# A two-layer hybrid trunk on one core: mixers in small parts between the projection matmuls, TensorE in program order

## The chip, the cores and the metric

The kernel runs on one core of a Trainium2 chip. The metric is the device time of one execution in microseconds, the median of three runs. A separate execution is recorded by the profiler; all views below come from it.

## The reference

A trunk of two layers on 256 tokens of width 1024. Each layer normalises its input, multiplies it with one wide weight and cuts the product into the inputs of three mixers (softmax differential attention, an SSD state space mixer in chunks of 128, and gated linear attention, GLA, in chunks of 64); their outputs, side by side, go through the output weight, then an FFN and a gate on a side input `p`.

```
for i in range(DEPTH):                          # DEPTH = 2
    a = rms_norm(h, attn_norm[i])
    proj = a @ w_in[i]
    (da_q, da_k, da_v, ssd_z, ssd_xbc, ssd_dt,
     gla_q, gla_k, gla_v, gla_g, gla_lr) = jnp.split(proj, IN_SPLITS, axis=-1)
    y_da = diff_attention(da_q, da_k, da_v, ...)    # rms norm and rope on q, k; two softmaxes, a difference
    y_ssd = ssd_mixer(ssd_z, ssd_xbc, ssd_dt, ...)  # conv of 4 taps, silu, decays, states of 2 chunks
    y_gla = gla_mixer(gla_q, gla_k, gla_v, gla_g, gla_lr, ...)  # log-sigmoid gates, cumulative sums, states of 4 chunks
    mix = jnp.concatenate([y_da, y_ssd, y_gla], axis=-1)
    h = h + mix @ w_out[i]
    f = rms_norm(h, ffn_norm[i])
    h = h + (silu(f @ w_ffn_gate[i]) * (f @ w_ffn_up[i])) @ w_ffn_down[i]
    h = h + sigmoid(h @ ple_w_gate[i]) * (p[i] @ ple_w_proj[i])
```

## The kernel before

Every matrix product is done in two halves of precision: a weight tile is loaded by DMA (`load_w`, L195 to L218), ScalarE copies its rounded part (`wh`, L213), VectorE subtracts to get the rest (`wl`, L214), and TensorE (PE) does three matmuls per pair of tiles (high by high, high by low, low by high). Activations have two halves in the same way.

The work is a list of units, one weight tile each. A layer has 19 input units in the order of the table `PLAN` (q, z, x, k, gq, gk, gv, sg, v, ple: the slices of `proj`; x0 to x3 are the inputs of SSD, gk and gq those of GLA), then four units o1 and two o2 for the output weight, 22 FFN units up with 16 down, and four gate units. In the input units with 512 columns per matmul the three matmuls stand on L836 to L838; z has 272 columns (L226 to L228); x and the output units use 256 columns (L244 to L246); the FFN is L238 and L240.

The mixers are Python generators: `da_gen` (attention), `ssd_gen`, `gla_gates_gen` and `gla_gen`. A `yield` ends a step; `step(S, names)` runs a generator to its next `yield`. `PLAN` names for each input unit the steps that are emitted whole ahead of the unit's own matmuls, and `PLAN_OUT` does so for the o1 units. The framework's scheduler then sets the order of each engine's instructions from these by its own costs, so PE's order in the program differs from the order of the text: mixer matmuls move between the projection matmuls. Each engine runs its list in order and waits at an instruction until what it needs is there.

PSUM's eight banks are divided: `NACC` = 5 for the accumulators of the units (`acc` tiles), 3 for the mixers (`pm` tiles).

Names that the text uses: `ssq` and L292, L295: the sum of squares and the PE matmul for the token norm. L706 to L712, L718: gates of GLA, `gk` and its cumulative sum. L553 to L558: convolution and SiLU of SSD. L651: the SSD product of B and C. L415 to L436: norm, rope and transposes of q and k (`qg`, `qh`, `ql`). L463 to L483: scores, their maximum `mx`, exponentials `e`. L755: GLA states (`gst`). L614 to L624: SSD outputs `xd`. L797, L805: GLA outputs.

Of the kernel before, what the change touches and what calls it, by code (L numbers as in the profile page):

```python
# [20 lines left out]
P = 128  # L21
# [12 lines left out]
BEFORE = False  # L34
NACC = 5
WSLOT = 2176
# [33 lines left out]


PLAN = [
    ('q0', ()),
# [7 lines left out]
    ('x3', ('gates',)),  # L81
    ('k0', ('gates', 'ssd', 'ssd')),
    ('k1', ('gates', 'ssd')),
    ('gk', ('da', 'da')),
    ('gv0', ('ssd', 'ssd')),
    ('gv1', ('gla', 'gla', 'da', 'da')),
    ('sg0', ('da', 'ssd')),
    ('sg1', ('gla', 'da')),
    ('v0', ('da', 'da', 'ssd', 'ssd')),
    ('v1', ()),  # L90
    ('ple', ('gla', 'da')),
]
PLAN_OUT = [('gla', 'da'), ('da',), (), ('da', 'da')]

# [13 lines left out]
def trunk_kernel(ctx: ExitStack, tc: tile.TileContext, a: dict):  # L108
    nc = tc.nc
    pe, dve, act, pool = nc.tensor, nc.vector, nc.scalar, nc.gpsimd  # L110

# [108 lines left out]
    split_at = []  # L220

    def product(out, pairs):

        n = len(pairs)
        for i, (sh, sl, mh, ml) in enumerate(pairs):
            pe.matmul(out, sh, mh, start=i == 0, stop=False)  # L226
            pe.matmul(out, sh, ml, start=False, stop=False)  # L227
            pe.matmul(out, sl, mh, start=False, stop=i == n - 1)  # L228

    def product_t(out, w, lo, x, ks, n, wide):  # L230


        if wide:

            pairs = list(zip(ks, w, strict=True))
            for p0 in range(0, len(pairs), 2):
                for k, (wh, _) in pairs[p0:p0 + 2]:
                    pe.matmul(out, wh[:, lo:lo + P], x[k], start=k == 0, stop=False)  # L238
                for k, (_, wl) in pairs[p0:p0 + 2]:
                    pe.matmul(out[:, :T], wl[:, lo:lo + P], x[k][:, :T], start=False, stop=k == n - 1)  # L240
            return
        for k, (wh, wl) in zip(ks, w, strict=True):
            sh, sl, hi = wh[:, lo:lo + P], wl[:, lo:lo + P], x[k][:, :T]
            pe.matmul(out, sh, hi, start=k == 0, stop=False)  # L244
            pe.matmul(out, sh, x[k][:, T:], start=False, stop=False)  # L245
            pe.matmul(out[:, :T], sl, hi, start=False, stop=k == n - 1)  # L246

    def gemm_t(blocks, x, wide=False, split=0, apart=False):
# [147 lines left out]
    def da_gen(i, S):  # L396
# [30 lines left out]
        for t in range(4):  # L427
# [9 lines left out]
            qk.append((qh, ql))  # L437
            if t == 1:
                yield
        yield  # L440
# [12 lines left out]
        for qb, heads in units:  # L453
            nh, nk = len(heads), P * (qb + 1)
            pb = [bank(), bank()]
            for j, hd in enumerate(heads):
# [3 lines left out]
                for n, (a_, b_) in enumerate(((0, 0), (0, 1), (1, 0))):  # L460
                    for c in range(2):
                        r = slice(64 * c, 64 * c + 64)
                        pe.matmul(pb[c][:, j * nk:(j + 1) * nk], q[a_][r, o + qb * P:o + (qb + 1) * P],  # L463
                                  k[b_][r, o:o + nk], start=j == 0 and n == 0, stop=False,
                                  skip_group_check=True)
            for c in range(2):
# [3 lines left out]
            if len(es_of) == 2:  # L470
                attn_t(es_of[0])
            mx = small("mx", [P, 2, 4])
# [33 lines left out]
        for qb in range(2):  # L506
            y = bank()
            for hd in range(4):
# [4 lines left out]
                else:  # L513
                    t = at[1 + hd // 2]
                    j = 2 * (hd % 2)
                    pe.matmul(o, t[:, j * P:(j + 1) * P], v[0][:, vs], start=True, stop=False)
                    pe.matmul(o, t[:, (j + 1) * P:(j + 2) * P], v[1][:, vs], start=False, stop=True)
            ys.append(head_norm(y))
            yield
# [41 lines left out]
    def ssd_gen(i, S):  # L561
# [18 lines left out]
        def decays(b):  # L580
            ms = []
            for g in range(2):
                pd = bank()
                for n, r in enumerate(rs[b][g]):
# [5 lines left out]
                                  cbm[:, o:o + P].unsqueeze(1).to_broadcast([P, 4, P]), ALU.mult)  # L590
                ms.append(m)
            return ms

# [14 lines left out]
        def rows(b, ms):  # L608
            py = bank()
            for hd in range(8):  # L610
                pe.matmul(py[:, hd * 64:(hd + 1) * 64], ms[hd // 4][:, (hd % 4) * P:(hd % 4 + 1) * P],
                          xdt[b][:, hd * 64:(hd + 1) * 64], start=True, stop=True)
            y = xd[b]
            dve.tensor_tensor(y, py, y, ALU.add)  # L614
# [37 lines left out]
        cbm = slot("cbm")  # L652
        dve.tensor_tensor(v3(cbm, 4), v3(pcb, 4), upper.unsqueeze(1).to_broadcast([P, 4, P]), ALU.mult)
        token_major(1)
        yield
# [7 lines left out]
        dve.tensor_tensor(v3(xe, 8), v3(xdt[0], 8), headed(ce[:, 0:8], 8), ALU.mult)  # L663
        m0 = decays(0)
        yield
# [5 lines left out]
        act.activation(st, pst, AF.Copy)  # L671
        rows(0, m0)
        rs.append(masked_dta(1))
# [7 lines left out]
        dve.tensor_tensor(xd[1], xd[1], ot, ALU.add)  # L681
        m1 = decays(1)
        yield
        rows(1, m1)
        yield
# [40 lines left out]
    def gla_gen(i, S):  # L726
# [5 lines left out]
        for j in range(2):  # L732
            for b in range(2):
                o = (2 * j + b) * P
                s = slice(j * T + b * P, j * T + (b + 1) * P)
                for e in range(2):
                    r = slice(64 * e, 64 * e + 64)
                    pe.matmul(pa[e][:, o:o + P], k[r, s], q[r, s], start=True, stop=True)
        for e in range(2):
            dve.copy_predicated(attm[e], gmask.unsqueeze(1).to_broadcast([P, 4, P]), v3(pa[e], 4))  # L740
# [11 lines left out]
        for j in range(2):  # L752
            for c in (0, 1, 2):
                b, r = c // 2, slice(64 * (c % 2), 64 * (c % 2) + 64)
                pe.matmul(pst[c][:, j * T:(j + 1) * T], kx[r, (2 * b + j) * P:(2 * b + j + 1) * P],  # L755
                          v[b][r, j * T:(j + 1) * T], start=True, stop=True)
        prev = [None]
        for c in range(3):
# [16 lines left out]
        for j in range(2):  # L775
            for b in range(2):
                o = (2 * j + b) * P
                for e in range(2):
                    hd = 2 * j + e
                    pe.matmul(po[e][:, o:o + P], attm[e][:, 2 * j + b], v[b][:, hd * P:(hd + 1) * P],  # L780
                              start=o == 0, stop=False, skip_group_check=True)
        for j in range(2):
            for c in range(1, 4):
                b, cc = c // 2, c % 2
                o, s = (2 * j + b) * P, j * T + c * 64
                for e in range(2):
                    r = slice(64 * e, 64 * e + 64)
                    pe.matmul(po[e][64 * cc:64 * cc + 64, o:o + P], q[r, s:s + 64],
                              prev[c][r, j * P:(j + 1) * P], start=False, stop=True,
                              skip_group_check=True)  # L790
        ys, sg = [], S["sg"]
        for e in range(2):
# [9 lines left out]
        for e in range(2):  # L802
# [3 lines left out]
            for j in range(2):  # L806
                parts(mx[2 * j + e], 0, pt[:, j * T:(j + 1) * T], gcol)
        yield

# [3 lines left out]

    def step(S, *names):
        for n in names:
            if n not in S["gens"]:
                S["gens"][n] = {"da": da_gen, "ssd": ssd_gen, "gates": gla_gates_gen, "gla": gla_gen}[n](S["i"], S)
            next(S["gens"][n], None)

    def in_units(i, S, x):  # L820
# [3 lines left out]
        def xunits(name, t, evac):  # L824

            def go(half):
                def f(w):
# [3 lines left out]
                    for k in range(4):  # L831
                        wh, wl = w[k]
                        kk_ = 4 * half + k
                        for b in range(2):
                            xh, xl = x[kk_][:, b * P:(b + 1) * P], x[kk_][:, T + b * P:T + (b + 1) * P]
                            pe.matmul(pb[b], xh, wh, start=kk_ == 0, stop=False)  # L836
                            pe.matmul(pb[b], xh, wl, start=False, stop=False)  # L837
                            pe.matmul(pb[b], xl, wh, start=False, stop=kk_ == KD - 1)  # L838
                    if half:
                        evac(pb)  # L840
# [101 lines left out]
    def out_units(i, S, x):  # L942

        def first(c2):
            def go(w):
                if c2 < 4:
                    step(S, *PLAN_OUT[c2])
                pb = gemm_t(lambda c: (w, c * P), S["mix"][1] + S["mix"][2])[0][0]
                hv = h[:, 2 * c2:2 * c2 + 2]
                dve.tensor_tensor(hv, v3(pb, 2), hv, ALU.add)  # L950
            return go
# [13 lines left out]
        for c2 in range(4):  # L965
            units.append((a["w_o1"][i, c2], KD, T, first(c2)))
        for c4 in range(2):
# [224 lines left out]
```

## Time and profile before

| | |
|---|---|
| median of three runs | 815.48 us (815.0 to 816.54) |
| profiled execution | 808.83 us |
| its span | 806.7 us |
| mean granted clock of PE | 0.991 |
| PE busy | 787.6 us (98% of the span) |
| PE weight loads busy | 701.5 us (87%) |
| VectorE (DVE) busy | 629.9 us (78%) |
| ScalarE (ACT) busy | 473.0 us (59%) |
| DMA | 134.92 MB, mean 167 GB/s |

Busy times are shares of the whole span, in which stages with different limits follow each other. A granted clock of 1.00 is 2.4 GHz, 0.50 is 1.2 GHz. The profiled execution lies outside the three timed runs, 6.65 us under their median.

### The profile page before, as it was taken

Reading aid. Unit: us, or ns where it says so; the run is one execution under the profiler, and the core shown is the slowest. Engines: PE = TensorE matmul, PEld = TensorE weight load, DVE = VectorE, ACT = ScalarE, POOL = GpSimd, SP = SyncE. Lnnn points to the kernel's source line nnn. Section 1 sums busy time; section 2 is a strip of 40 time slices with the busy share of each in tenths; the row PEclk is TensorE's granted clock in tenths of the full one; section 3 lists DMA queues with packets and bytes.
Section 4 is the critical chain, followed back from the end, with each engine's and each line's share of the span. In section 5 each row is a group of like instructions: output and inputs, shape, how many; then the busy total and the mean of one; then the engine's idle time right before and its main releaser. Section 6 shows DMA issues by size and latency. Waiting matters only on the chain.

```text
span 806.7 us, 13158 instructions
## 1 busy us (share of the span) xinstructions
PE 787.6 (98%) x5034; PEld 701.5 (87%) x5034; DVE 629.9 (78%) x1297; ACT 473.0 (59%) x822; POOL 22.8 (3%) x36
## 2 busy tenths in 40 slices
PE   8999989899999999999999999898999999999997
PEld 6998867899888888888999987688998888888897
DVE  5999988888887777667789699687888777766673
ACT  7768557546665565545667655284566565555461
POOL 2000000002000000000010000000020000000000
PEclk9999999999999999999999999799999999999999
DMA  8763323434565553657555531432445555445541
GB/s 285 286 216 132 145 105 106 157 110 152 209 209 178 188 176 115 207 182 261 189 184 175 197 118 53 141 125 102 157 160 197 199 180 205 143 151 189 196 157 53
DMA packets 24013, 134.92 MB, mean 167 GB/s; under 512 B 2960, under 2 KB 4752, under 8 KB 11408
## 3 DMA queue, kind: packets, MB, share of 16 engines
q1 hardware_dynamic: 23616, 133.57, 48.0%
q8 instruction: 39, 0.64, 0.3%
q0 software_dynamic: 192, 0.52, 0.2%
q14 instruction: 22, 0.18, 0.1%
q10 hardware_dynamic: 144, 0.01, 0.0%
HBM read 133.05 MB, written 1.05 MB: 166 GB/s over the span
## 4 chain that ended last, share of the span: by engine, by line
PE 86%; DVE 8%; ACT 2%; DMA 2%; issue 1%; SPq 0%; ACTq 0%; DVEq 0%
PE acc L238 30%; PE acc L240 15%; PE acc L246 8%; PE acc L245 7%; PE acc L244 7%; PE acc L836 3%; PE acc L838 3%; PE acc L837 2%; DVE wl L214 2%; PE acc L226 1%; PE acc L227 1%; PE acc L228 1%; DMA h<-in_x 1%; PE pm L755 1%; PE pm L463 1%
## 5 line engine op out<-in xcount | busy, mean ns | idle before, releaser
L213 ACT ACTIVATE wh<-st 128x1024 fp32r<-128x1024 f32 (+5 forms) x274 | 267.1, 979 | 233.6 <-PE acc L238 91.7
L214 DVE TENSOR_TENSOR wl<-st,wh 128x1024 fp32r<-128x1024 f32 (+5 forms) x274 | 307.8, 1129 | 108.5 <-ACT wh L213 108.1
L238 PE MATMUL acc<-x,wh 128*128 128x512 f32 x704 | 222.0, 396 | 0.1
L240 PEld LDWEIGHTS acc<-x,wl 128*128 128x128 f32 x704 | 132.2, 188 | 31.2
L240 PE MATMUL acc<-x,wl 128*128 128x256 f32 x704 | 138.4, 278 | 0.0
L238 PE MATMUL acc<-act,wh 128*128 128x512 f32 x352 | 111.8, 395 | 0.0
L238 PEld LDWEIGHTS acc<-x,wh 128*128 128x128 f32 x704 | 107.3, 189 | 0.7 <-DVE x L275 0.7
L246 PE MATMUL acc<-x,wl 128*128 128x256 f32 x320 | 90.6, 283 | 0.9 <-DVE wl L214 0.9
L244 PE MATMUL acc<-x,wh 128*128 128x256 f32 x320 | 90.8, 284 | 0.0
L245 PE MATMUL acc<-x,wh 128*128 128x256 f32 x320 | 90.5, 283 | 0.0
L240 PEld LDWEIGHTS acc<-act,wl 128*128 128x128 f32 x352 | 66.2, 188 | 14.3
L240 PE MATMUL acc<-act,wl 128*128 128x256 f32 x352 | 72.0, 279 | 0.0
L836 PE MATMUL acc<-wh,x 128*128 128x512 f32 x160 | 65.8, 414 | 0.4 <-ACT wh L213 0.4
L837 PE MATMUL acc<-wl,x 128*128 128x512 f32 x160 | 64.8, 405 | 0.2 <-DVE wl L214 0.2
L838 PE MATMUL acc<-wh,x 128*128 128x512 f32 x160 | 64.7, 404 | 0.0
L246 PEld LDWEIGHTS acc<-x,wl 128*128 128x128 f32 x320 | 61.1, 191 | 1.1 <-DVE wl L214 1.1
L244 PEld LDWEIGHTS acc<-x,wh 128*128 128x128 f32 x320 | 61.1, 191 | 0.2
L245 PEld LDWEIGHTS acc<-x,wh 128*128 128x128 f32 x320 | 61.1, 191 | 0.1
L244 PE MATMUL acc<-mix,wh 128*128 128x256 f32 x192 | 54.5, 288 | 1.5 <-ACT ple L915 1.5
L238 PEld LDWEIGHTS acc<-act,wh 128*128 128x128 f32 x352 | 54.9, 189 | 1.3
L245 PE MATMUL acc<-mix,wh 128*128 128x256 f32 x192 | 54.8, 287 | 0.0
L246 PE MATMUL acc<-mix,wl 128*128 128x256 f32 x192 | 54.5, 286 | 0.0
(268 smaller groups left out, 1177.6 us busy)
## 6 DMA issues: line engine op xcount, KB each, us to landing
st<-in_w_f SPq DMA_DIRECT2D x44, 1024.0 KB, 4.9
st<-in_w_d SPq DMA_DIRECT2D x32, 704.0 KB, 4.1
st<-in_w_x SPq DMA_DIRECT2D x18, 1024.0 KB, 4.9
st<-in_w_o SPq DMA_DIRECT2D x12, 1024.0 KB, 4.9
st<-in_w_t SPq DMA_DIRECT2D x11, 1024.0 KB, 4.9
st<-in_w_g SPq DMA_DIRECT2D x8, 1024.0 KB, 5.1
st<-in_w_z SPq DMA_DIRECT2D x3, 1088.0 KB, 5.0
st<-in_w_x SPq DMA_DIRECT2D x8, 256.0 KB, 5.0
```

The source lines that it names most:

```text
L213: i_hi = act.activation(wh[:, s], st[:, o], AF.Copy)
L214: i_lo = dve.tensor_tensor(wl[:, s], st[:, o], wh[:, s].bitcast(F32), ALU.subtract)
L226: pe.matmul(out, sh, mh, start=i == 0, stop=False)
L227: pe.matmul(out, sh, ml, start=False, stop=False)
L238: pe.matmul(out, wh[:, lo:lo + P], x[k], start=k == 0, stop=False)
L240: pe.matmul(out[:, :T], wl[:, lo:lo + P], x[k][:, :T], start=False, stop=k == n - 1)
L244: pe.matmul(out, sh, hi, start=k == 0, stop=False)
L245: pe.matmul(out, sh, x[k][:, T:], start=False, stop=False)
L246: pe.matmul(out[:, :T], sl, hi, start=False, stop=k == n - 1)
L836: pe.matmul(pb[b], xh, wh, start=kk_ == 0, stop=False)
L837: pe.matmul(pb[b], xh, wl, start=False, stop=False)
L838: pe.matmul(pb[b], xl, wh, start=False, stop=kk_ == KD - 1)
```

## The change

- `pe` becomes a wrapper: every matmul and transpose is kept in program order, so the scheduler no longer moves PE instructions against each other. (All PE rows then carry the wrapper's lines, L117 and L121.) The other engines are still scheduled.
- The generators get more stops, `yield 'part'`, within a step. A function `tick` advances the first pending step by one part; it is called after every second group of three matmuls with 256 columns and after every group of three with 512. `spread` puts a unit's steps into the pending list, runs the unit and then finishes what is left. A `'-'` in the plan is a turn in which nothing is emitted.
- `PLAN` and `PLAN_OUT` are new, and the first o1 unit multiplies its first four tiles for both halves of the output before the rest (`split=4`).
- `NACC` is 4: four banks for the units, four for the mixers.

```diff
-NACC = 5
+NACC = 4
...
-    ('k0', ('gates', 'ssd', 'ssd')),
+    ('k0', ('gates', 'ssd')),
...
-PLAN_OUT = [('gla', 'da'), ('da',), (), ('da', 'da')]
+PLAN_OUT = [('-', 'da'), ('-', '-', 'da'), ('-', '-', 'da'), (), (), ()]
...
-    pe, dve, act, pool = nc.tensor, nc.vector, nc.scalar, nc.gpsimd
+    dve, act, pool = nc.vector, nc.scalar, nc.gpsimd
+
+    class pe:
+
+        @staticmethod
+        def matmul(*args, **kw):
+            return tc.keep_in_program_order(nc.tensor.matmul(*args, **kw))
...
+    pending = []
+
+    def tick():
+        if pending:
+            S, name = pending[0]
+            if name == '-' or step(S, name):
+                pending.pop(0)
...
             pe.matmul(out, sl, mh, start=False, stop=i == n - 1)
+            if i % 2:
+                tick()
...
             for c in range(2):
 
                 pe.matmul(v3(pb[c], nh)[:, :, nk - P:], idb, negb.unsqueeze(1).to_broadcast([P, nh, P]),
                           start=False, stop=True, skip_group_check=True)
             if len(es_of) == 2:
+                yield 'part'
                 attn_t(es_of[0])
...
-    def step(S, *names):
-        for n in names:
-            if n not in S["gens"]:
-                S["gens"][n] = {"da": da_gen, "ssd": ssd_gen, "gates": gla_gates_gen, "gla": gla_gen}[n](S["i"], S)
-            next(S["gens"][n], None)
+    def step(S, n):
+
+        if n not in S["gens"]:
+            S["gens"][n] = {"da": da_gen, "ssd": ssd_gen, "gates": gla_gates_gen, "gla": gla_gen}[n](S["i"], S)
+        return next(S["gens"][n], None) != 'part'
+
+    def spread(S, names, go, w):
+        pending.extend((S, n) for n in names)
+        go(w)
+        while pending:
+            tick()
...
                             pe.matmul(pb[b], xl, wh, start=False, stop=kk_ == KD - 1)
+                            tick()
...
-            units.append((*tile_, lambda w, go=go, steps=steps: (step(S, *steps), go(w))))
+            units.append((*tile_, lambda w, go=go, steps=steps: spread(S, steps, go, w)))
```

In the rows of the program's order below, tile numbers differ between the two kernels, since they count allocations; the same tile is meant where the words say so.

PE at the start of layer 0, before: `acc_346` is the second bank of unit z0, `pm_287` the token norm of the input.

```order
L226 MATMUL acc_346<-wh_229,x_148 128x272
L227 MATMUL acc_346<-wl_230,x_148 128x272
L228 MATMUL acc_346<-wh_229,x_148 128x272
L226 MATMUL acc_346<-wh_237,x_158 128x272
L295 MATMUL pm_287<-ones,ssq_191 128x1 x2
L227 MATMUL acc_346<-wl_238,x_158 128x272
L228 MATMUL acc_346<-wh_237,x_158 128x272
```

PE at the same place, changed: `acc_203` is the last bank of q1, `acc_319` the first of z0.

```order
L117 MATMUL acc_203<-wh_171,x_181 128x512
L117 MATMUL acc_203<-wl_172,x_181 128x512
L117 MATMUL acc_203<-wh_171,x_181 128x512
L117 MATMUL pm_287<-ones,ssq_191 128x1 x2
L117 MATMUL acc_319<-wh_229,x_125 128x272
L117 MATMUL acc_319<-wl_230,x_125 128x272
L117 MATMUL acc_319<-wh_229,x_125 128x272
L117 MATMUL acc_319<-wh_229,x_132 128x272
L117 MATMUL acc_319<-wl_230,x_132 128x272
```

The token-norm matmul has moved from the middle of z0's second bank to ahead of the whole unit.

ScalarE at the gates of GLA in layer 0, before: `ge` (lines 708 to 710) is the gate on its way to `gk`, `conv_857` the last convolution of SSD, L558 its SiLU; `wh` are weight copies.

```order
L553 ACTIVATE conv_857<-xp_854,par_70 128x256 x2
L708 ACTIVATE ge_880<-pm_877 128x512
L213 ACTIVATE wh_1033<-st_1032 128x1024
L709 ACTIVATE ge_880<-ge_880 128x512
L710 ACT_TABLE_LOAD
L710 ACTIVATE ge_880<-ge_880 128x512
L213 ACTIVATE wh_1038<-st_1032 128x1024
L558 ACT_TABLE_LOAD
L558 ACTIVATE conv_857<-conv_857 128x512
```

The same place, changed: the gate's lines are 745 to 747, the SiLU's 587.

```order
L582 ACTIVATE conv_857<-xp_854,par_70 128x256 x2
L745 ACTIVATE ge_885<-pm_882 128x512
L674 ACT_TABLE_LOAD
L674 ACTIVATE ce_897<-pm_894 128x16
L746 ACTIVATE ge_885<-ge_885 128x512
L224 ACTIVATE wh_1033<-st_1032 128x1024
L587 ACT_TABLE_LOAD
L587 ACTIVATE conv_857<-conv_857 128x512
L747 ACT_TABLE_LOAD
L747 ACTIVATE ge_885<-ge_885 128x512
```

The SiLU and its table load stood behind the gate's last function and stand ahead of it now; the exponential `ce` of SSD has moved behind the gate's first one.

VectorE at the maximum of the first attention scores in layer 0, before: `mx_1383` is that maximum, `pm_1355` and `pm_1356` the scores, `xd` SSD outputs.

```order
L624 TENSOR_SCALAR xd_897<-xd_897,yf_1177 128x256 x2
L214 TENSOR_TENSOR wl_1347<-st_1345,wh_1346 128x1024
L214 TENSOR_TENSOR wl_1352<-st_1345,wh_1351 128x1024
L214 TENSOR_TENSOR wl_1468<-st_1466,wh_1467 128x1024
L214 TENSOR_TENSOR wl_1473<-st_1466,wh_1472 128x1024
L214 TENSOR_TENSOR wl_1563<-st_1561,wh_1562 128x1024
L475 TENSOR_REDUCE mx_1383<-pm_1355 128x4
L475 TENSOR_REDUCE mx_1383<-pm_1356 128x4
L614 TENSOR_TENSOR xd_925<-pm_1408,xd_925 128x512
L476 TENSOR_SCALAR mx_1383<-mx_1383 128x8
L615 TENSOR_TENSOR xd_925<-xd_925,sz_317 128x512
```

The same place, changed: the maximum is `mx_1435`, of scores `pm_1398` and `pm_1399`; `rs_t` and `yf` are the rsqrt chain of the second SSD output, `xd_985`.

```order
L225 TENSOR_TENSOR wl_1563<-st_1561,wh_1562 128x1024
L202 TENSOR_TENSOR rs_t_1380<-yf_1378 128x2
L203 SCALAR_TENSOR_TENSOR rs_t_1380<-rs_t_1380,rs_v_1379 128x2
L204 SCALAR_TENSOR_TENSOR yf_1378<-rs_t_1380,yf_1378 128x2
L202 TENSOR_TENSOR rs_t_1380<-yf_1378 128x2
L203 SCALAR_TENSOR_TENSOR rs_t_1380<-rs_t_1380,rs_v_1379 128x2
L204 SCALAR_TENSOR_TENSOR yf_1378<-rs_t_1380,yf_1378 128x2
L657 TENSOR_SCALAR xd_985<-xd_985,yf_1378 128x256 x2
L502 TENSOR_REDUCE mx_1435<-pm_1398 128x4
L502 TENSOR_REDUCE mx_1435<-pm_1399 128x4
L503 TENSOR_SCALAR mx_1435<-mx_1435 128x8
```

The second SSD output's product, rsqrt chain and scaling now come ahead of the maximum; before they came behind it.

## Rows read from the trace of the kernel before

**Rows 1.** PE's waits, whole run: line, releaser, us in total, times, longest.

```profile
PE pm L755 <- DVE mx L476: 4.1, 2, 2.1
PE pm L805 <- DVE fyn L797: 3.2, 2, 1.6
...
PE pm L651 <- ACT conv L558: 1.5, 2, 0.8
...
PE acc L244 <- ACT ple L915: 1.5, 2, 0.8
```

**Rows 2.** Windows: length, busy PE, PEld, DVE, ACT, POOL; granted clock, DMA share, GB/s.

```profile
72.00:112.00 40.00, 38.86 (x257) 33.01 (x255) 38.44 (x96) 22.52 (x36) 0.00 (x0) 1.00 0.24 86
...
511.70:521.90 10.20, 10.20 (x27) 7.25 (x27) 6.77 (x28) 3.27 (x11) 0.00 (x0) 0.50 0.01 2
556.05:559.50 3.45, 3.45 (x18) 3.45 (x17) 2.30 (x7) 1.87 (x4) 0.00 (x0) 0.51 0.59 249
```

**Rows 3.** Timeline of PE, layer bounds: start, us, engine, line, op, tiles, count.

```profile
62.81 0.40 PE L706 MATMUL pm<-w2r,lrt 128*128 128x256 f32 x2
...
194.70 0.63 PE L238 MATMUL acc<-x,wh 128*128 128x512 f32 x2
...
455.90 0.40 PE L706 MATMUL pm<-w2r,lrt 128*128 128x256 f32 x2
...
593.93 0.63 PE L238 MATMUL acc<-x,wh 128*128 128x512 f32 x2
```

**Rows 4.** Timeline of PE at the start of layer 0.

```profile
18.40 0.41 PE L226 MATMUL acc<-wh,x 128*128 128x272 f32 x2
...
24.95 0.29 PE L228 MATMUL acc<-wh,x 128*128 128x272 f32 x1
...
26.07 0.29 PE L228 MATMUL acc<-wh,x 128*128 128x272 f32 x1
...
33.06 0.60 PE L306 MATMUL pm<-cst,rcol 128*128 128x128 f32 x4
```

**Rows 5.** Timeline of DVE at the start of layer 0: the last ssq sum.

```profile
23.21 0.41 DVE L292 TENSOR_TENSOR ssq<-ssq 128x256 f32<-128x256 f32 x1
```

**Rows 6.** Timeline of PE, the wide matmuls of a k unit.

```profile
71.41 0.39 PE L836 MATMUL acc<-wh,x 128*128 128x512 f32 x1
...
72.32 0.39 PE L837 MATMUL acc<-wl,x 128*128 128x512 f32 x1
```

**Rows 7.** Timeline of ACT around the GLA gate.

```profile
69.92 0.63 ACT L710 ACTIVATE ge<-ge 128x512 f32<-128x512 f32 x1
...
71.52 1.28 ACT L558 ACT_TABLE_LOAD   x1
72.82 0.63 ACT L558 ACTIVATE conv<-conv 128x512 f32<-128x512 f32 x1
```

**Rows 8.** Timeline of DVE from the gate to the maximum of the scores.

```profile
70.59 0.69 DVE L712 SCALAR_TENSOR_TENSOR gk<-pm,ge 128x512 f32<-128x512 f32 x1 [0.58 <-ACT ge L710]
...
100.20 0.28 DVE L422 TENSOR_TENSOR qg<-rope,rope 128x128 f32<-128x128 f32 x1
...
103.31 0.68 DVE L589 TENSOR_TENSOR m<-m,cbm 128x512 f32<-128x512 f32 x1
...
105.49 0.14 DVE L193 SCALAR_TENSOR_TENSOR yf<-rs_t,yf 128x2 f32<-128x2 f32 x1
...
108.31 0.60 DVE L624 TENSOR_SCALAR xd<-xd,yf 128x256 f32<-128x256 f32 x2
...
116.31 0.16 DVE L476 TENSOR_SCALAR mx<-mx 128x8 f32<-128x8 f32 x1
```

**Rows 9.** Timeline of PE: the GLA state matmuls, with idle time before them.

```profile
116.54 1.10 PE L755 MATMUL pm<-gv,kx 64*128 64x256 f32 x4 [2.07 <-DVE mx L476]
```

**Rows 10.** Timeline of ACT: first and last of eight exponentials.

```profile
116.58 0.37 ACT L480 ACTIVATE e<-pm,mx 128x128 f32<-128x128 f32 x1 [6.39 <-DVE mx L476]
...
119.00 0.40 ACT L480 ACTIVATE e<-pm,mx 128x128 f32<-128x128 f32 x1
```

More of the change, by code (lines that the diff above doesn't have):

```diff
@@ L81 @@
     ('x3', ('gates',)),
-    ('k0', ('gates', 'ssd', 'ssd')),
[L83 to L87, printed above, removed]
+    ('k0', ('gates', 'ssd')),
+    ('k1', ('gates', '-', '-', 'ssd', 'ssd')),
+    ('gk', ('da', 'da', 'ssd')),
+    ('gv0', ('ssd',)),
+    ('gv1', ('gla', 'da', 'da', 'gla')),
+    ('sg0', ('ssd', 'da')),
     ('sg1', ('gla', 'da')),
-    ('v0', ('da', 'da', 'ssd', 'ssd')),
-    ('v1', ()),
-    ('ple', ('gla', 'da')),
+    ('v0', ('ssd', 'da', 'da')),
+    ('v1', ('gla', 'ssd')),
+    ('ple', ('da', '-', '-', 'da', 'gla')),
 ]
-PLAN_OUT = [('gla', 'da'), ('da',), (), ('da', 'da')]
+PLAN_OUT = [('-', 'da'), ('-', '-', 'da'), ('-', '-', 'da'), (), (), ()]
 def _two_pi_parts():
@@ L109, in trunk_kernel, with transpose @@
     nc = tc.nc
-    pe, dve, act, pool = nc.tensor, nc.vector, nc.scalar, nc.gpsimd
+    dve, act, pool = nc.vector, nc.scalar, nc.gpsimd
[3 more added lines that the diff above has]
+            return tc.keep_in_program_order(nc.tensor.matmul(*args, **kw))
+        @staticmethod
+        def transpose(*args, **kw):
+            return tc.keep_in_program_order(nc.tensor.transpose(*args, **kw))
     cp = ctx.enter_context(tc.tile_pool(name="const", bufs=1))
@@ L437, in da_gen @@
             qk.append((qh, ql))
-            if t == 1:
-                yield
+            if t < 3:
+                yield None if t == 1 else 'part'
         yield
@@ L470, in da_gen @@
             if len(es_of) == 2:
+                yield 'part'
                 attn_t(es_of[0])
@@ L517, in da_gen @@
                     pe.matmul(o, t[:, (j + 1) * P:(j + 2) * P], v[1][:, vs], start=False, stop=True)
+                if hd == 1:
+                    yield 'part'
             ys.append(head_norm(y))
@@ L591, in decays @@
                 ms.append(m)
+                if g == 0:
+                    yield 'part'
             return ms
@@ L612, in rows @@
                           xdt[b][:, hd * 64:(hd + 1) * 64], start=True, stop=True)
+                if hd == 3:
+                    yield 'part'
             y = xd[b]
@@ L653, in ssd_gen @@
         dve.tensor_tensor(v3(cbm, 4), v3(pcb, 4), upper.unsqueeze(1).to_broadcast([P, 4, P]), ALU.mult)
+        yield 'part'
         token_major(1)
@@ L663, in ssd_gen @@
         dve.tensor_tensor(v3(xe, 8), v3(xdt[0], 8), headed(ce[:, 0:8], 8), ALU.mult)
-        m0 = decays(0)
+        yield 'part'
+        m0 = yield from decays(0)
         yield
@@ L671, in ssd_gen @@
         act.activation(st, pst, AF.Copy)
-        rows(0, m0)
+        yield 'part'
+        yield from rows(0, m0)
         rs.append(masked_dta(1))
@@ L681, in ssd_gen @@
         dve.tensor_tensor(xd[1], xd[1], ot, ALU.add)
-        m1 = decays(1)
+        yield 'part'
+        m1 = yield from decays(1)
         yield
-        rows(1, m1)
+        yield from rows(1, m1)
         yield
@@ L738, in gla_gen @@
                     pe.matmul(pa[e][:, o:o + P], k[r, s], q[r, s], start=True, stop=True)
+        yield 'part'
         for e in range(2):
@@ L756, in gla_gen @@
                           v[b][r, j * T:(j + 1) * T], start=True, stop=True)
+            if j == 0:
+                yield 'part'
         prev = [None]
@@ L781, in gla_gen @@
                               start=o == 0, stop=False, skip_group_check=True)
+            yield 'part'
         for j in range(2):
@@ L790, in gla_gen @@
                               skip_group_check=True)
+            if j == 0:
+                yield 'part'
         ys, sg = [], S["sg"]
@@ L945, in go @@
             def go(w):
[L946 to L950, printed above, removed]
+                for pb, lo, hi in gemm_t(lambda c: (w, c * P), S["mix"][1] + S["mix"][2],
+                                         split=0 if c2 else 4):
+                    hv = h[:, 2 * c2 + lo:2 * c2 + hi]
+                    dve.tensor_tensor(hv, v3(pb, hi - lo), hv, ALU.add)
             return go
@@ L965, in out_units @@
         for c2 in range(4):
-            units.append((a["w_o1"][i, c2], KD, T, first(c2)))
+            units.append((a["w_o1"][i, c2], KD, T,
+                          lambda w, go=first(c2), c2=c2: spread(S, PLAN_OUT[c2], go, w)))
         for c4 in range(2):
```

5 lines of the change are left out of this document (added).

## The prediction

> **What bounds the kernel now.** I read the table of PE's waits first. TensorE is at work nearly all the time, and its few waits lie in the mixers: 4.1 us before the GLA state matmuls (L755), 3.2 before the last GLA transposes (L805), 1.5 before the SSD chunk product (L651), 1.5 at the first output unit (L244) [rows 1]; these are four of the table's ten rows, and none of the ten stands on a line of the FFN. So outside the mixers PE's own order of work sets the time, and a reordering there can gain nothing.
>
> Then the windows [rows 2]. From 72 to 112 us VectorE is busy 38.44 of 40.00 us, PE 38.86: two engines run at their limit side by side, and PE stays ahead of VectorE only because the order lets it do projections meanwhile. The other two rows show the clock: it was granted at 0.50 for 10.20 us and at 0.51 for 3.45 us. These are the two stretches that follow the waits at L755 and L805 in layer 1; the same two waits in layer 0 kept the full clock.
>
> What that costs is read from the layers [rows 3]. From the gate matmul after unit x3 to the first FFN matmul layer 0 takes 194.70 - 62.81 = 131.89 us, layer 1 593.93 - 455.90 = 138.03. The work is the same, so the two falls cost 6.14, or 3.07 each. The profiled execution took 808.83, 6.65 under the median of the timed runs, 815.48; that is about one more pair of falls, which I read but can't show. At full clock all through, the kernel before would take 808.83 - 6.14 = 802.7, and the sum starts there; about 13 of the median's 815.5 would then be clock.
>
> **The change, part by part.** No instruction is added or removed: the lists of PE rows hold equal numbers of matmuls. What changes is who stands behind whom, and PE, in program order, now waits wherever the text puts a matmul too early.
>
> *Start of layer 0.* The token-norm matmul (pm<-ones,ssq) stood inside z0's second bank and now stands ahead of all of z0. It needs the last ssq sum, which VectorE ends at 23.21 + 0.41 = 23.62 [rows 5], and VectorE's order there is unchanged. PE is done with q1 at 18.40 [rows 4] and so waits 5.2 us. Part is made good: z0's and x0's weights are ready by then, so their 96 matmuls run at the plain pitch, (26.07 - 24.95)/9 = 0.124 [rows 4], from 24.1 to 36.0, where x0 ended at 33.06 before: +2.9, in layer 0 alone (in layer 1 and the FFN the row stands where it did).
>
> *The gate's cumulative sum.* PE's cst,gk matmul now comes behind 27 of the 38 wide matmuls that stood between the gate matmul and 72.32. At their pitch of (72.32 - 71.41)/4 = 0.2275 [rows 6] PE gets there at 72.32 - 10 x 0.2275 = 70.0. Its input gk ended at 70.59 + 0.69 = 71.28 [rows 8]. On ScalarE the SiLU of the last convolution, with its table load, now stands ahead of the logarithm that gk needs: 1.28 + 0.63 [rows 7], pipelined 1.8. So gk is there at 73.1 and PE waits 3.1, where it waited 0.8 for that SiLU.
>
> *The query transposes and the scores.* These are set by VectorE, so I go by VectorE's clock and don't add waits one by one. Up to the rotated query (qg, 100.20 + 0.28 [rows 8]) its list holds the same work in both kernels, and it is saturated: PE can't pass the transposes sooner than 100.5. But PE has by then been given nine wide matmuls and twelve small ones less, about 3.2 us, so that much of its time is lost, whatever the wait at gk took of it. From there to the scores' maximum (mx, ended at 116.31 + 0.16) VectorE took 16.0 us. Now it does more ahead of mx: an xd scaling of two halves (0.60), one m product and one xd product (0.68 each), and eight small steps of the rsqrt chains (0.14 each alone, half that between others) [rows 8]. That is 2.4 to 3.1, so mx is ready at 118.9 or later. Four exponentials, one each (119.00 - 116.58)/7 = 0.346 [rows 10], then free the bank that the third GLA state matmul takes: 118.9 + 0.1 + 1.4 = 120.4. Before, PE passed 116.54 [rows 9] with four wide matmuls and two state matmuls less done, 1.1 us of work. So at this place it is late by 120.4 - 116.54 - 1.1 = 2.8 per layer, all of the above included. If the 1.8 by which gk is late idles VectorE too, it is 4.6. I take 3.5, nearer to the count that rests on rows alone. Behind the waiting matmul stand all projections of sg1 and the scores of the second query block, so nothing covers it.
>
> *Behind it.* Walking the new order on with durations of before, I find waits of 1.2 (second score bank behind a GLA state copy), 2.0 (the transposes of e behind the SSD outputs' four evictions) and 3.0 (at the end, as at L805 before), together 6.2 against 1.6 + 0.8 in layer 0 before [rows 1]: +3.8. This walk is weak, as it gives PE about 4 us less to do than the trace has; that surplus may fill the gaps. Ends: 0 and +3.8; taken: +2.0.
>
> *Four accumulator banks for five, four mixer banks for three.* An FFN unit's bank comes back two units later, so a whole unit of matmuls covers its eviction, and no wait on an FFN line exists now: 0. If that cover failed at each of the 44 up units by one small matmul's pitch it would be 44 x 0.124 = 5.5, the far end. The fourth mixer bank removes waits only where a bank is what is missing; L651, L805 and L244 wait for data.
>
> *Clock.* Four waits of 1.6 to 2.1 were followed by two falls, 3.07 each. The new order has the start and four more per layer of at least 1.6 in my walk, nine: at that rate 9 x 0.5 x 3.07 = 13.8. A PE at half clock in a stretch that VectorE sets loses less, so I take half, 6.9, with ends 0 and 13.8.
>
> Sum: 802.7 + 2.9 + 2 x (3.5 + 2.0) + 6.9 = 823.5, against the profiled 808.83 and the median 815.48.
>
> **Rivals.**
> *Faster.* The small parts do what parts can do: the surplus of projections fills every gap behind the scores, and without idle stretches at full length the clock holds. For it: PE's later waits are data chains of 1 to 2 us that six wide matmuls cover. Against: the two VectorE dates above don't depend on parts. 802.7 + 2.9 + 2 x 1.0 = 807.6; this also covers the case that the scores' maximum gets its turn earlier than the listed order lets me expect.
> *No change.* The scores cost 2.8 per layer, later waits are as before, and one or two falls remain: 802.7 + 2.9 + 5.6 + 4.0 = 815.2.
> *Slower still.* Every upper end: 4.6 + 3.8 per layer and 13.8 of clock: 802.7 + 2.9 + 16.8 + 13.8 = 836.2. It decides from the point where VectorE idles for gk.
> *The clock swings.* Waits return every few microseconds, and each is followed by a fall like the shorter one seen (3.45 us at half clock, 1.7 lost [rows 2]): seven per layer, 14 x 1.7 = 23.8 in place of 6.9: 840. The Trainium skill ("TensorE: Matmul & The Clock Gate", section "A second HAM failure mode: psum-queue depth-cycling") describes such a case: a kernel that cycles through accumulator banks pauses briefly between groups of matmuls often enough that the clock goes back and forth, with matmuls of normal length at full clock and throughput lost between. The trace before agrees only in that falls came after short waits; half of them brought none.
>
> **How the numbers follow.** Forecast 0.53 (its own range 817 to 831), faster 0.17, no change 0.08, slower still 0.17, swinging clock 0.05. About 0.2% is what a measurement of this kernel tells from no change: 813.9 to 817.1. Faster 0.17, same 0.08, slower 0.75. The range from 811 to 838 leaves out most of the fast rival (some 0.12) and the tail above (0.08).
>
> **What would show it.** In the changed kernel's waits: ssq ahead of a norm matmul, about 5 us, once; gk from VectorE, 3 us, twice; qg and the exponentials' bank, 1 to 3 us per layer; and granted clocks near 0.5 in the stretches behind some of them. The layers from x3's end to the FFN should take at least 137 us each even at full clock. If PE idles under 6 us per layer there, or z0 starts at 18.4, the forecast is wrong; if the waits are there and the clock stays full, only the last term is.

## The result, and the profile after

The changed kernel takes 840.46 us (median of four runs, 839.44 to 844.28), the kernel before 815.24 beside it: ratio 1.0335, 95% interval 1.027 to 1.040. Slower was right; 840.46 lies above the range (811 to 838), and the loss of 25 is three times the forecast's 8. Ratios here compare runs at like clock; beside e13 and e14 that leaves four of the thirteen runs of the kernel before, 802.70 to 809.96.

The page's first part and the table of PE's waits, changed kernel (line, releaser, us in total, times, longest). All PE lines are now the wrapper's; the releaser tells the place:

```profile
PE 797.2 (95%) x5034; PEld 702.1 (84%) x5034; DVE 634.7 (76%) x1299; ACT 477.4 (57%) x824; POOL 22.8 (3%) x36
```

```profile
PE pm L121 <- DVE mix L413: 7.1, 2, 3.6
PE pm L117 <- DVE gk L749: 7.0, 2, 3.5
PE pm L117 <- DVE ssq L316: 5.4, 1, 5.4
PE pm L121 <- DVE qg L446: 4.7, 2, 2.4
PE pm L117 <- ACT e L507: 3.8, 2, 1.9
PE pm L117 <- ACT v L915: 1.8, 2, 0.9
```

PE does the same matmuls, but instead of 98% it is busy 95% of a longer span. Four of these six waits are the ones forecast by place and nearly by length: ssq 5.4 (5.2), gk 3.5 (3.1), qg 2.4 and the exponentials e 1.9. The first row, the transposes behind the SSD output's evictions (mix), was walked at 2.0 and is 3.6.

The same bounds of the layers as [rows 3], from the end of x3 to the first FFN matmul:

```profile
67.72 0.40 PE L117 MATMUL acc<-wh,x 128*128 128x512 f32 x1
...
216.50 0.63 PE L117 MATMUL acc<-x,wh 128*128 128x512 f32 x2
...
477.70 0.40 PE L117 MATMUL acc<-wh,x 128*128 128x512 f32 x1
...
625.77 0.63 PE L117 MATMUL acc<-x,wh 128*128 128x512 f32 x2
```

Layer 0 takes 148.78 us where it took 131.89, layer 1 148.07. With the start, late by 67.72 - 62.81 = 4.9, that is 4.9 + 16.9 + 16.2 = 38.0 above the kernel before at full clock, 802.7: 840.7, against 840.95 of this execution. Nothing is lost outside the start and the mixers' two stretches, where the forecast looked for it.

Windows of the changed kernel on its seven stretches of low clock (columns as in [rows 2]):

```profile
22.40:29.20 6.80, 6.20 (x29) 6.20 (x30) 5.99 (x18) 4.02 (x9) 0.00 (x0) 0.53 0.61 213
79.80:83.20 3.40, 3.40 (x10) 2.61 (x10) 3.40 (x6) 1.31 (x3) 0.00 (x0) 0.54 0.02 5
131.20:141.40 10.20, 10.20 (x31) 5.77 (x32) 5.76 (x20) 2.20 (x9) 0.00 (x0) 0.50 0.28 104
155.00:158.40 3.40, 3.40 (x10) 2.68 (x9) 0.62 (x3) 3.15 (x10) 0.00 (x0) 0.52 0.00 0
489.80:493.20 3.40, 3.40 (x9) 2.66 (x9) 3.40 (x6) 1.30 (x3) 0.00 (x0) 0.52 0.00 0
547.00:550.40 3.40, 3.40 (x15) 2.46 (x14) 2.82 (x9) 1.06 (x1) 0.00 (x0) 0.60 0.03 7
561.40:568.20 6.80, 5.50 (x15) 4.54 (x16) 2.51 (x8) 5.13 (x14) 0.00 (x0) 0.50 0.00 0
```

They add up to 37.4 us; each begins in or right behind one of the waits (ssq, gk, e, mix in layer 0; gk, gst, mix in layer 1). At half speed that is up to 18.7 us of matmul time. For layer 0 an account by length closes: its nine waits sum to 14.1 against 5.6 before, +8.5, and its three stretches cost 17.0/2 = 8.5; together 17.0, measured 16.9.

VectorE from the gate to the scores' maximum, changed kernel, to set against [rows 8]:

```profile
77.81 0.69 DVE L749 SCALAR_TENSOR_TENSOR gk<-pm,ge 128x512 f32<-128x512 f32 x1 [2.66 <-ACT ge L747]
...
97.78 0.16 DVE L194 TENSOR_SCALAR rs_v<-yss 128x2 f32<-128x2 f32 x1
97.85 0.68 DVE L634 TENSOR_TENSOR r<-cst,dtah 128x512 fp32r<-128x512 f32 x1
...
107.75 0.28 DVE L446 TENSOR_TENSOR qg<-rope,rope 128x128 f32<-128x128 f32 x1
...
124.08 0.17 DVE L194 TENSOR_SCALAR rs_v<-yss 128x2 f32<-128x2 f32 x1 [1.04 <-ACT ysq L652]
124.28 0.17 DVE L198 TENSOR_SCALAR yf<-rs_v 128x2 int32<-128x2 int32 x1
124.48 0.17 DVE L199 TENSOR_SCALAR yf<-yf 128x2 int32<-128x2 int32 x1
...
129.32 0.17 DVE L503 TENSOR_SCALAR mx<-mx 128x8 f32<-128x8 f32 x1
```

Counted from x3's end the rotated query comes at 40.3 (before 37.7), since VectorE itself stood idle for the gate, 2.66 us where it was 0.58. From there to the maximum it takes 129.49 - 108.03 = 21.5 us where it took 16.0. The rsqrt chain's steps, each on the one before, start 0.20 apart (124.08, 124.28, 124.48), not the 0.07 to 0.14 that I priced them at from a place where other work lay between (97.78 to 97.85 above shows such a step), and the chain waited 1.04 for its input.

PE at the GLA state matmul that needs the bank of the exponentials:

```profile
131.08 1.10 PE L117 MATMUL pm<-gv,kx 64*128 64x256 f32 x2 [1.92 <-ACT e L507]
```

### The profile page after: what moved, and what is told of

Its sections match the earlier page's. It is cut to its first block, busy times and chain, and to the rows that moved or that the text cites. A ratio compares the mean times of both kernels' runs of the same rounds, so it can differ in the third digit from the quotient of the medians.

```text
span 838.5 us, 13176 instructions
## 1 busy us (share of the span) xinstructions
PE 797.2 (95%) x5034; PEld 702.1 (84%) x5034; DVE 634.7 (76%) x1299; ACT 477.4 (57%) x824; POOL 22.8 (3%) x36
## 5 line engine op out<-in xcount | busy, mean ns | idle before, releaser
L117 PE MATMUL acc<-x,wh 128*128 128x512 f32 (+1 forms) x1344 | 338.8, 343 | 0.1
L117 PE MATMUL acc<-x,wl 128*128 128x256 f32 x1024 | 228.8, 279 | 0.0
L117 PEld LDWEIGHTS acc<-x,wl 128*128 128x128 f32 x1024 | 193.6, 189 | 31.2
L117 PEld LDWEIGHTS acc<-x,wh 128*128 128x128 f32 x1344 | 207.2, 190 | 1.1 <-DVE x L299 0.7
L117 PE MATMUL acc<-wh,x 128*128 128x512 f32 (+1 forms) x448 | 153.2, 399 | 0.1
L117 PE MATMUL acc<-act,wh 128*128 128x512 f32 x352 | 111.8, 395 | 0.0
L117 PEld LDWEIGHTS acc<-wh,x 128*128 128x128 f32 x448 | 87.1, 203 | 16.8 <-issue 2.9
L117 PE MATMUL acc<-wl,x 128*128 128x512 f32 (+1 forms) x224 | 86.4, 386 | 0.5 <-DVE wl L225 0.5
L117 PEld LDWEIGHTS acc<-act,wl 128*128 128x128 f32 x352 | 66.2, 188 | 14.3
L117 PE MATMUL acc<-mix,wh 128*128 128x256 f32 x384 | 71.5, 286 | 1.2 <-ACT mix L412 0.8
L117 PE MATMUL acc<-act,wl 128*128 128x256 f32 x352 | 72.0, 279 | 0.0
L117 PEld LDWEIGHTS acc<-mix,wh 128*128 128x128 f32 x384 | 60.0, 191 | 2.5 <-DVE mix L413 1.3
L117 PEld LDWEIGHTS acc<-act,wh 128*128 128x128 f32 x352 | 54.9, 189 | 1.3
L117 PE MATMUL acc<-mix,wl 128*128 128x256 f32 x192 | 54.3, 283 | 0.0
L117 PEld LDWEIGHTS acc<-wl,x 128*128 128x128 f32 x224 | 45.6, 204 | 5.5 <-DVE wl L225 1.1
L304 DVE TENSOR_TENSOR gu<-acc,gu 128x256 f32<-128x256 f32 x88 | 36.7, 417 | 2.9 <-ACT gu L303 2.9
L117 PEld LDWEIGHTS acc<-mix,wl 128*128 128x128 f32 x192 | 36.8, 191 | 0.0
L311 POOL TENSOR_TENSOR ssq<-ssq,sq 128x512 f32<-128x512 f32 x12 | 18.7, 1557 | 526.5 <-ACT sq L308 526.3
L303 ACT ACTIVATE gu<-acc 128x256 f32<-128x256 f32 x88 | 32.0, 366 | 1.8 <-PE acc L117 1.8
L298 ACT ACTIVATE x<-h,par 128x256 fp32r<-128x256 f32 x32 | 15.2, 500 | 17.3 <-DVE h L1010 8.9
```

The source lines that it names most:

```text
L117: return tc.keep_in_program_order(nc.tensor.matmul(*args, **kw))
L298: act.activation(hi, h[:, c], AF.Copy, scale=g)
L303: act.activation(out, pb[:, T:], AF.Copy)
L304: dve.tensor_tensor(out, pb[:, :T], out, ALU.add)
L311: pool.tensor_tensor(acc, acc, sq, ALU.add)
```

## The experiments

Theory A was: the fixed order makes PE wait for dates that VectorE and ScalarE set, and each wait brings a stretch at half clock. Fourteen runs (e10 is the kernel before once more), each in three rounds with the kernel before beside it; medians, and differences to 840.46 unless said otherwise. Four executions of one kernel lie up to some 5 us apart, so differences of 2 to 3 us, as in e1 and e2, stand near the noise.

**e1, the token norm behind z0 in layer 0.**

```diff
-            S["rcol"] = token_norm(S["acc"])
...
+                if half == 0 and i == 0:      # behind both banks of z0
+                    S["rcol"] = token_norm(S["acc"])
...
```

> The changed kernel with one matmul moved in layer 0: the token-norm matmul stands behind both banks of z0 instead of ahead of the unit (z0's evictions behind it). Theory A (what a wait of TensorE costs is its length plus half of the stretch at half clock behind it): the wait of 5.35 us on ssq goes, the half-clock stretch from 22 to 29 us goes with it, x3 ends near 63 instead of 67.7; time 840.5 - 5 = 835.5. Rival B (the clock falls come anyway, somewhere else): the wait alone is saved, 837.5. In both the layers behind keep their 148 to 149 us.

837.17 (834.99 to 840.43), -3.3. The wait on ssq went, but z0 then waited 2.20 us for its own low weights, and the clock still fell, for 3.4 us (22.0 to 25.4, granted 0.54) where it was 6.8:

```profile
20.21 0.39 PE L117 MATMUL acc<-wl,x 128*128 128x272 f32 x1 [2.20 <-DVE wl L225]
```

Nearer to B: what the wait held back in part came again as another wait and another fall.

**e2, the gate's sum later in the plan.**

```diff
-    ('k1', ('gates', '-', '-', 'ssd', 'ssd')),
+    ('k1', ('-', '-', '-', '-', '-', 'gates', 'ssd', 'ssd')),
```

> The changed kernel with the cumulative sum of the GLA gate five turns later in the plan (k1: five empty turns, gates, ssd, ssd). Theory A: the wait for gk (3.51 us per layer) and the falls behind it (some 3 us at half clock each) go: 2 x (3.5 + 1.5) = 10, 830.5. Rival V (a date that VectorE sets is what counts, since VectorE itself idles 2.66 us for the same gate): the query transposes still come at about 40 us behind x3, PE's wait there grows from 2.4 to 5 us, and the time falls by the clock stretches at most: 837 to 840.5.

837.90 (836.11 to 841.07), -2.6: V's time, and outside theory A's 830.5. The wait for gk is gone, and these rows of its wait table are new or took its place:

```profile
PE pm L121 <- DVE ot L716: 3.6, 2, 1.8
PE pm L117 <- DVE xe L697: 2.9, 2, 1.5
...
PE pm L121 <- DVE qg L446: 1.4, 2, 0.7
PE pm L117 <- DVE r L634: 1.3, 4, 0.4
```

V was wrong on the place: the wait did not grow at the query (0.7 where 2.4 was) but moved to the SSD steps that now stand closer together.

**e3, the scores ahead of the SSD output.**

```diff
-    ('sg0', ('ssd', 'da')),
+    ('sg0', ('da', 'ssd')),
```

> The changed kernel with the two names of unit sg0 exchanged (da, ssd instead of ssd, da): the first scores' maximum comes ahead of the second SSD output's rsqrt chain on VectorE. Theory A with VectorE's dates: the maximum, 21.5 us behind the rotated query now, comes about 17 us behind it; the wait for the exponentials (1.9 us) and the 10 us at half clock behind it in layer 0 go; the SSD output is later, so the wait of 3.6 us on its evictions may grow. Saved: 2 to 5 per layer, 831 to 836. Rival (the maximum is late because PE is): no change within 1 us.

830.01, -10.5, a little more than expected. Counted from the rotated query the maximum ends 3.4 us earlier, the wait on the exponentials shrinks from 1.9 to 0.3 and the stretch of 10.2 us behind it is gone:

```profile
126.02 0.17 DVE L503 TENSOR_SCALAR mx<-mx 128x8 f32<-128x8 f32 x1
```

```profile
PE pm L117 <- ACT e L507: 0.6, 2, 0.3
```

**e4, the waits filled with matmuls of no use.**

```diff
+    def junk(out, n, src=None):
+        src = ident.bitcast(BF16) if src is None else src
+        for _ in range(n):
+            pe.matmul(out[:, :2 * P], src[:, :P], src, start=True, stop=True)
...
+        junk(pb, 27)        # ahead of the gate's sum; likewise at four more places
```

> The changed kernel with matmuls of no use in five places right ahead of the matmuls that wait (128x256 bf16 on constants, into a bank that the waiting step then overwrites): 40 before the token norm of layer 0, and per layer 27 before the gate's cumulative sum, 20 before the query transposes, 15 before the GLA state matmuls, 27 before the first transposes of attention weights; they fill about the waits' lengths and leave the dates as they are. Theory A (the stretches at half clock come of the idle time before them): the clock stays full behind these places, 37 us at half clock go, and the time falls by 14 to 18, to 822.5 to 826.5. Rival B (the falls come of something else in these stretches, or cost nothing because other engines set the pace): within 3 us of 840.5, or slower by the useless work.

828.86, -11.6: theory A, though it expected 14 to 18. The window over the whole run:

```profile
0.00:826.00 826.00, 806.51 (x5252) 711.87 (x5252) 634.18 (x1299) 477.29 (x824) 22.82 (x36) 1.00 0.47 163
```

The clock is full throughout, so the stretches did come of the idle time, and with no other change of the kernel they cost 11.6. That is less than half of 37.4: at full clock PE gets to the next date sooner and waits there, as I read it. The other 26 us against 802.7 are dead time, filled or not: 13.6 us of waits are left (the first one of the program, 1.5, not counted) and the 218 useless matmuls take some 24 at 0.11 each, against 11.8 of waits in the kernel before. (With PE's list longer, the scheduler also moved some of VectorE's instructions, so the dates are not quite those of the changed kernel.)

**e5, PE given back to the scheduler; e6, the kernel before in program order.**

```diff
-            return tc.keep_in_program_order(nc.tensor.matmul(*args, **kw))    # e5; e6 puts the wrapper into the kernel before
+            return nc.tensor.matmul(*args, **kw)
...
```

> The changed kernel (parts, ticks, new plan, four and four banks) with TensorE given back to the scheduler: the wrapper no longer keeps the program order. Theory O (the fixed order is what makes TensorE wait: the text puts matmuls ahead of their inputs): the waits shrink towards those of the kernel before, 815 to 822. Rival P (the new plan puts the mixers' work at worse dates on VectorE and ScalarE, whatever TensorE's order): the waits for gk, the scores' maximum and the SSD evictions stay, 832 to 840.

> The kernel before (whole steps, old plan, five and three banks) with TensorE in program order and nothing else. Theory O: whole steps stand ahead of their units with nothing between their matmuls, so TensorE waits for VectorE and ScalarE within each step; slower than the changed kernel, 845 to 880, and the parts and the plan of the change win a share of that back. Rival P: the order as such costs little, 815 to 825, and it is the plan that lost the time.

e5: 809.0, -31.5, and a little faster than the kernel before (ratio 0.9941, interval 0.9915 to 0.9967). e6: 870.1, +55.6 on the kernel before. First rows of the wait tables, e5 and then e6:

```profile
PE pm L117 <- ACT e L507: 5.0, 2, 2.5
PE pm L117 <- ACT v L915: 3.4, 2, 1.7
PE pm L121 <- DVE fyn L840: 3.3, 2, 1.6
```

```profile
PE pm L116 <- ACT conv L569: 15.0, 2, 7.5
PE pm L116 <- DVE r L614: 13.9, 2, 7.0
PE pm L120 <- DVE fyn L808: 9.0, 2, 4.5
```

Theory O, in both. The fixed order of whole steps costs 55.6; the rest of the change wins back 30 of it (870.1 to 840.5), of which the fourth mixer bank has 9 (e8) and parts, turns and the new plan 20.6. In e5 the waits of the norm's and the mixers' matmuls on ssq, gk, qg and mix are gone without any change of plan. What parts and plan are worth without the fixed order is read against e7 below, the kernel before with four and four banks: 809.0 against 808.63, nothing. The gain of e5 on the kernel before is no more than that of the bank alone.

**e7, four and four banks in the kernel before; e8, five and three in the changed one.**

```diff
-NACC = 5        # e7; e8 the other way
+NACC = 4
```

> The kernel before with four accumulator and four mixer banks in place of five and three, nothing else. By every theory that I hold the FFN units don't miss the fifth bank: no wait on an FFN line, and 813 to 817. If the fifth bank mattered, waits for evictions appear on the FFN lines (44 units up), up to 5.5 us.

> The changed kernel with five accumulator and three mixer banks, as before the change, nothing else. TensorE's order stays as it is, word for word. Theory A: with three banks the mixers' matmuls wait for evictions more often (the waits on ql, the exponentials and the SSD evictions are waits for a bank); 843 to 855. Rival (four accumulator banks hurt the units): faster than 840.5.

e7: 808.63 against 814.52, ratio 0.9941 (0.9911 to 0.9971); no wait on an FFN line. e8: 849.47, +9.0. The fourth mixer bank is worth something in both orders; I had priced it at 0. e7's own profile has some 20 us at half clock, so part of its gain may lie in which stretches fall; the two were not separated.

**e9, the SiLU behind the gate's logarithm.**

```diff
-        act.activation(o, o, AF.Silu)
+        if t < 3:
+            act.activation(o, o, AF.Silu)
...
+        act.activation(xbc[3], xbc[3], AF.Silu)    # at the start of ssd_gen
```

> The changed kernel with the SiLU of the last convolution given to ScalarE behind the gate's logarithm again (at the start of the SSD generator); TensorE's order is the same, word for word. Theory V (the gate's date comes from ScalarE, and VectorE and TensorE both wait for it): gk comes 1.8 us earlier, the wait for it shrinks from 3.5 to about 1.7 per layer, VectorE idles 1.8 less and the rotated query comes that much earlier too; saved 1.8 per layer, and 1.5 more where the fall behind it goes: 834 to 837. Rival (VectorE's own work sets the query's date): the wait for gk shrinks and the wait for the query grows by as much, 839 to 840.5.

833.11, -7.4, V and more: the wait for gk is 1.6 (3.5), that on qg 2.0 (2.4), and no stretch of low clock follows the gate in either layer. One ScalarE function with its table load in another place, PE's program order untouched:

```profile
PE pm L121 <- DVE qg L446: 4.0, 2, 2.0
PE pm L117 <- DVE gk L751: 3.1, 2, 1.6
```

**e10, the kernel before again.**

> The kernel before, unchanged, for a second profile. My reading was that the first profile (808.83) holds one pair of falls of the clock in layer 1 (13.65 us at half clock) and the median of the timed runs one pair more. If that holds, a profile at 813 to 816 has some 27 us at half clock, in both layers; if a profile at 814 or more has 14 us or less, the difference is something else.

814.78; the profile is of an execution of 815.84. Its windows of low clock:

```profile
116.00:129.20 13.20, 13.20 (x33) 8.82 (x34) 7.30 (x29) 4.73 (x22) 0.00 (x0) 0.51 0.10 42
163.80:167.20 3.40, 3.40 (x19) 3.40 (x18) 2.28 (x6) 1.83 (x4) 0.00 (x0) 0.52 0.65 270
518.60:528.80 10.20, 10.20 (x27) 7.31 (x28) 6.78 (x28) 3.48 (x12) 0.00 (x0) 0.52 0.01 2
562.40:566.00 3.60, 3.41 (x20) 3.44 (x20) 2.51 (x7) 1.80 (x4) 0.00 (x0) 0.63 0.65 262
```

30.4 us in both layers, as the reading said. Here all four places fell, in the first profile two. Of the runs of the kernel before beside e13 and e14, one took 802.70 at a mean clock of 0.999: the 802.7 at full clock that the forecast had worked out.

**e11 and e12, the two places of e7 and e5 filled.**

```diff
+        junk(pst[0], 16)              # ahead of the GLA state matmuls
...
+            if e == 0:
+                junk(pt, 16)          # ahead of the last GLA transposes
```

> The kernel before with four and four banks, and 16 matmuls of no use (128x256 bf16) in each layer ahead of the GLA state matmuls and 16 ahead of the last GLA transposes, the two places behind which the clock fell (19 us at half clock in the run with four and four banks alone, 808.6). Theory A (falls come of the idle time): the falls go, 9.5 us are saved, and the useless work costs what of 64 x 0.11 = 7.0 us isn't idle time now (5.7 at these places): 798 to 803. Rival B: the falls stay, 808 to 812.

> The changed kernel with TensorE given back to the scheduler, as in e5 (809.0), with the same 2 x 16 matmuls of no use per layer. It had 11 us at half clock behind these places. Theory A: 809.0 - 5.5 and up to 1 us of useless work that isn't idle time now: 803 to 806. Rival B: 808 to 812.

e11: 808.70 (e7 808.63), the time of B. e12: 814.44 (e5 809.0), slower than either theory had it. In e11 the wait at the state matmuls is gone (that at the last transposes, 1.7, is not) and the low clock is down from 20.5 to 10.2 us, but a new and longer wait stands behind the filled one, and the clock falls there:

```profile
PE pm L468 <- DVE gst L773: 5.7, 2, 2.9
```

In e12 the first filling missed its wait: the scheduler's order has the 16 useless matmuls at 114.8 to 116.6 us, and the state matmul that waits for the exponentials comes later, idle from 119.3 to 122.1, 2.8 us where e5 had 2.5:

```profile
PE pm L117 <- ACT e L512: 5.6, 2, 2.8
```

So e12 says nothing on theory A, only that useless work beside a wait costs time. That filling a wait moves the idle time on to the next place is shown by one case, e11; in e4's fixed order no wait over 1.3 us was left, beside the program's first, and the clock stayed full.

**e13, the edits of e1, e3 and e9 together, in the fixed order; e14, the same with PE given back to the scheduler.** (The diff is that of e1, e3 and e9, in e14 with e5's.)

> The changed kernel in its fixed order with the three single edits together: token norm behind z0, the SiLU behind the gate's logarithm, the scores ahead of the SSD output. Alone they saved 3.3, 7.4 and 10.5 us. If these places are separate (each a date that TensorE waits for, and the fall behind it): 840.5 - 21 = 819. If a mended place only uncovers the next wait (the evictions of the SSD output, 3.6 us, are next in line): 825 to 830.

> The run with TensorE given back to the scheduler (809.0) with the same three edits. If the three are faults of the plan, they help here too: 800 to 806. If they hurt only because the order is fixed, since the scheduler moves other matmuls into these places: 807 to 812.

e13: 822.59, -17.9, of the 21.2 that the three saved singly: between the two expectations. What is left is led by the mix wait, 7.5 us in all, the evictions that the second expectation named. e14: 803.69 (800.11 to 807.32, ten runs), ratio to the kernel before 0.9952 (0.9913 to 0.9991): a little faster than it, than e5 by 5.3 and than e7 by 4.9. Its first waits:

```profile
PE pm L117 <- DVE xd L649: 2.5, 2, 1.3
PE pm L121 <- DVE fyn L842: 2.1, 2, 1.0
PE pm L117 <- ACT v L917: 1.8, 2, 0.9
```

No wait over 1.3 us is left among these, and its profile has one stretch of low clock, 118 to 125 us. So the plan has faults of its own, which help in either order when mended.

## Why the prediction was wrong

The direction, the places and the start of the sum held. Two steps of the sum failed, both in size: the scores' dates on VectorE (3.5 per layer, measured 8.5 in layer 0) and the clock (6.9, measured 11.6 by e4 and 17.3 by the account of the trace).

**What bounds the kernel, and the start of the sum** held: 802.7 at full clock is a time that a run reached (802.70), and the median's other 13 us go with the four falls of e10, whose waits are those of the first profile. The 0.2% that was to tell a change from none was too narrow: the kernel before alone took 802.7 to 817.6 over all comparisons.

**Start of layer 0**, +2.9: measured 4.9. The stretch of low clock behind the wait holds some 6 us of PE's work, so 2 to 3 us of the 4.9 are clock, and the step's size at full clock roughly holds (2.0 to 2.9). e1 shows that z0 couldn't have used all of that time.

**The gate's sum** held: 3.5 for 3.1. e9 shows the larger part of its cause, the SiLU on ScalarE: with it out of the way 1.6 are left. The exponential `ce` with its table load, which also moved in between the gate's functions, was left out of the forecast; no run separates it.

**The scores**, 3.5 per layer by VectorE's dates, was mis-sized. PE passed that place 131.08 - 67.72 = 63.4 us behind x3; before it was 53.7, and with 1.1 for the work in between 54.8. So 8.5 late, beyond even the upper end, 4.6. VectorE's dates make up all of it: 2.6 at the rotated query (I had VectorE's idling with the gate as the upper end, 1.8, and not in the value), 5.5 for 2.4 to 3.1 from there to the maximum, and 1.5 from the maximum to the matmul as foreseen, less the 1.1. Two terms failed, then: the idling and the chain's price. e3 shows that this piece of order was the dearest.

**The later waits**, +2.0: behind that place layer 0 waits 5.7 us against 2.4 before, +3.3, inside the ends. The mix wait alone was 3.6 for 2.0, and the end 0.6 where 3.0 was expected.

**The clock**, 6.9, was mis-sized as well. "At that rate 9 x 0.5": the rate came from one execution, 6.65 us under the median, and e10 shows four falls for four waits in an ordinary one. I had the number that said so further up (13 us for four waits, 3.2 each) and used the other; with it the halved term would have been 14.4 and the sum 831. In the changed kernel seven stretches followed ten waits of 1.2 us or more. By the account by length the clock took the start's 2.0, 8.5 in layer 0 and 13.6/2 = 6.8 in layer 1: 17.3 for 6.9, beyond its end of 13.8. With 17.3, the start at 2.9 and 8.5 and 9.7 per layer of net waiting (layer 1's waits sum to 15.3) the sum is 802.7 + 2.9 + 18.2 + 17.3 = 841.1.

e4 measures the clock in another way, and it gives less: without the falls the time is 11.6 lower, inside the ends. By that count the waits hold the greater miss, 26.2 us above 802.7 where the forecast had 2.9 + 2 x 5.5 = 13.9 and at most 19.7. The two counts differ because time that PE gains at full clock before a date of VectorE's turns into waiting for it, as I read it. So the missing 17 us lie in two steps, the scores' dates and the clock, and both were set too low; how they divide is not settled.

**Four banks**, 0: the FFN part held; the mixers' gained (e7, e8), so this term pulled the other way and did not cause the miss.

**The rivals.** "Slower still", 836.2, was the nearest in its way, by both its ends: it was to decide where VectorE idles for gk, and VectorE did. "The clock swings", 840, had the time but not the way: seven stretches in 840 us, behind some of the longer waits, not fourteen. The Trainium skill's case of it ("TensorE: Matmul & The Clock Gate", "A second HAM failure mode: psum-queue depth-cycling") agrees with this trace in so far as short pauses of PE were followed by swings between the two levels, seven times in 838.5 us; no run here separates bank cycling from plain waits for data.

## What to carry to other kernels

Fixing an engine's order can turn the dates of the others into waits, here ten of 1.2 us or more; before doing so, list those dates (the other engines' saturated stretches, not just the one chain) and put each waiting instruction behind them, or leave that engine to the scheduler and mend the plan alone (809.0 against 840.5 here, 803.7 with three mends). Test the parts of a bundled change singly: one line, the fourth mixer bank, gave the kernel before as much (808.6) as the whole change gave under the scheduler (809.0). A wait of TensorE costs more than its length where the clock falls behind it, so take the rate of falls from the median's distance to the full-clock time, not from one profile. When useless work is put into a wait, look in the trace whether it stands in the wait at all (e12) and whether the idle time only moves on (e11).

## What the runs showed of the hardware

The stretches of low clock lasted 3.4 to 10.2 us in the changed kernel and 3.4 to 13.2 in the kernel before. The clock did not fall behind each wait: behind the 2.4 us on qg it held in both layers of the changed kernel, yet fell in layer 1 of e3, and the state copies' 1.2 us was followed by a fall. The kernel before took from 802.7 to 817.6 us over these comparisons with its program unchanged; the runs listed with their clocks go from 0.999 (802.70) over 0.991 (808.10) to 0.980 (816.60). A chain of dependent small VectorE steps (128x2) runs at 0.20 us a step, and at 0.07 to 0.08 where other work lies between.
